# Attention scores as two fp32r matmuls of 128 rows in a hybrid decoder block

## The chip, the cores and the metric

The kernel runs on one core of one Trainium2 chip. The metric is the device time of one execution in microseconds, lower is better. TensorE is PE in the profile (its weight loads are PEld), VectorE is DVE, ScalarE is ACT, GpSimd is POOL, and SyncE, which here only issues transfers, is SP.

## The reference

One decoder block on 512 tokens of width 2048, all in float32: RWKV-7 time mixing and sliding-window attention side by side, merged by gates, then a gated convolutional feed-forward. What the change touches is the attention:

```python
q = rms_norm(q.reshape(B, S, 16, 64), q_gain)
k = rms_norm(k.reshape(B, S, 4, 64), k_gain)
qb = q.reshape(B, nb, 128, 4, 4, 64)          # 4 blocks of 128 tokens, 4 key heads, 4 query heads each
kb, vb = band(k), band(v)                     # each block sees its own 128 keys and the 128 before
scores = jnp.einsum('bnqhgd,bnkhd->bnhgqk', qb, kb) * 64 ** -0.5
scores = jnp.where(valid, scores + alibi, NEG_BIG)
p = jax.nn.softmax(jnp.concatenate([scores, sink], -1), -1)[..., :-1]
o = jnp.einsum('bnhgqk,bnkhd->bnqhgd', p, vb)
```

A score contracts over 64 channels of a head.

## The kernel before

The large matmuls run in fp32r, a form of float32 in which TensorE passes once over the data with a shortened mantissa. Every large operand is therefore split in two: a high part, rounded to fp32r by ACT (`act.activation(hi, src, AF.Copy)`), and a low part, the rest, by DVE (`lo = src - hi`). `load_w` does so for weights (L245 and L246: `whi`, `wlo` from `raw`), `split` for other tiles (L208 and L209 of the kernel before). A projection tile, `ztile`, has 16 chunks of 128 channels with three matmuls each (L262, L263, L264: high times high, high times low, low times high), 128 by 512 elements, into one accumulator `acc`.

The attention stands between 45 and 265 us of the span. It begins with the key and value tiles. `qk_norm` takes a finished accumulator: DVE scales it into `zq` (L410), ACT squares it into `sqq` (L412), four small matmuls sum the squares (`head_stats`, L376), DVE works out the inverse root in a dozen small steps (`rq`), a transpose on PE (L379) and a trip through memory spread it over the rows (`rsb`), and `finish` (L405) multiplies, one tile later, so that the trip is hidden. Its result is `kn` for keys, `qn` for queries: two heads of 64 channels in the two halves of the 128 rows. Each key head is then copied by transfers on ACT's queue (L430) into both halves of its own tile `kd`, so that a query head finds its keys in its own half.

There are four head groups (one key head and four query heads, in two query tiles). `queries(g + 1)` is written ahead of the attention of group g, so that the projections of the next group fill TensorE while the softmax of this one runs; the last group has a gate projection and the following stage's projections instead. For each of the four blocks of a group, L469 makes the scores of its four heads: plain float32, 64 rows (`hs`), in PSUM tiles `scp0` and `scp1`, one for each half of the rows. The program has four such matmuls for a block; a float32 matmul leaves two records in the profile. DVE adds the position bias (L475, `sc`), takes the maximum (L480), ACT exponentiates (L486, `pr`), PE transposes (L495), ACT and DVE copy (L497, L499, `pT`), PE multiplies by the values (L503), DVE scales (L506, `ot`), PE transposes again (L509), ACT copies (L510).

The order on each engine comes from the framework's scheduler, which places instructions by its own estimate of their durations; only what is wrapped in `pin` keeps its written order. POOL's queue carries sums of weights for later stages (L230, `s_o`), each waiting for its first half to land.

Of the kernel before, what the change touches and what calls it, by code (L numbers as in the profile page):

```python
# [8 lines left out]
F32 = mybir.dt.float32  # L9
F32R = mybir.dt.float32r  # L10
F16 = mybir.dt.float16
I32 = mybir.dt.int32
AF = mybir.ActivationFunctionType
ALU = mybir.AluOpType
# [4 lines left out]
P = 128  # L19
S = 512  # L20
NT = S // P
HD = 64
C = 64
NCH = S // C
BLK = 128
# [111 lines left out]
def block_kernel(ctx: ExitStack, tc: tile.TileContext, d: Dims, a: dict, out: bass.AP):  # L137
    nc = tc.nc
    act, dve, pool, pe, sync = nc.scalar, nc.vector, nc.gpsimd, nc.tensor, nc.sync
# [41 lines left out]
    qgs = cstp.tile([P, 1], F32, name="qgs")  # L181
# [25 lines left out]
    def split(hi, lo, src, pin=free):  # L207
        pin(act.activation(hi, src, AF.Copy))  # L208
        pin(dve.tensor_tensor(lo, src, hi.bitcast(F32) if hi.dtype == F32R else hi, op=ALU.subtract))  # L209
# [73 lines left out]
    if True:  # L283
# [107 lines left out]
        with ExitStack() as pt:  # L391
            ap_ = pt.enter_context(tc.tile_pool(name="att", bufs=1, reuse_waits="tile"))
            sps = pt.enter_context(tc.tile_pool(name="sc_ps", bufs=1, space=PSUM, reuse_waits="tile"))
            mps = pt.enter_context(tc.tile_pool(name="mi_ps", bufs=3, space=PSUM, reuse_waits="tile"))

            def small():
                return mps.tile([P, S], F32, name="mi", tag="mi")

            unscaled = []

            def finish():

                if unscaled:
                    dst, z, rb, then = unscaled.pop()
                    pin(dve.tensor_tensor(dst, z, rb, op=ALU.mult))  # L405
                    then()

            def qk_norm(acc, gain, dst, then=lambda: None):
                z = ap_.tile([P, S], F32, name="zq", tag="zq", bufs=3)
                dve.tensor_scalar(z, acc, gain, None, op0=ALU.mult)  # L410
                sq = ap_.tile([P, S], F32, name="sqq", tag="sqq", bufs=2)
                act.activation(sq, acc, AF.Square)  # L412
                ps = small()
                head_stats(ps, sq)
                rs = rsqrt_small(ap_, ps[:, 0 : 2 * NT], 1.0 / HD, RMS_EPS)
                rb = head_rows(ap_, small(), rs, bufs=2)
                finish()
                unscaled.append((dst, z, rb, then))

            NHK = d.KVD // HD  # L420
            kd = [ap_.tile([P, S], F32, name=f"kd{h}") for h in range(NHK)]
            vt = ap_.tile([P, NT, d.KVD], F32, name="vt")
            for t in range(NKV):
                acc = ztile(d.c_ka + t * P)
                kn = ap_.tile([P, S], F32, name="kn", tag="kn", bufs=2)

                def copies(t=t, kn=kn):
                    for h in range(2):
                        for e in range(2):
                            act.dma_start(kd[2 * t + h][e * HD : (e + 1) * HD], kn[h * HD : (h + 1) * HD])  # L430

                qk_norm(acc, col("kg"), kn, copies)
                acc = ztile(d.c_va + t * P)
                vf = ap_.tile([P, S], F32, name="vf", tag="zq", bufs=3)
                act.activation(vf, acc, AF.Copy)
                ps = small().rearrange("p (n c) -> p n c", c=P)
                for b in range(NT):
                    pe.transpose(ps[:, b], vf[:, b * P : (b + 1) * P], ident)
                act.activation(vt[:, :, t * P : (t + 1) * P], ps, AF.Copy)

            GQ = d.HQ // NHK

            def queries(g):
                qn = []
                for j in range(GQ // 2):
                    acc = ztile(d.c_q + (g * GQ // 2 + j) * P)
                    q = ap_.tile([P, S], F32, name=f"qn{j}", tag=f"qn{j}", bufs=2)
                    qk_norm(acc, qgs, q)
                    qn.append(q)
                return qn  # L450

            nxt = queries(0)
            for g in range(NHK):
                qn = nxt
                if g + 1 < NHK:
                    nxt = queries(g + 1)
                else:
                    emit_gate()
                    finish()
                oT = ap_.tile([P, GQ // 2, S], F32, name="oT", tag="oT", bufs=2)  # L460
                for n in range(NT):
                    ts = slice(n * P, (n + 1) * P)
                    k0 = 0 if n else BLK
                    nk = 2 * BLK - k0
                    scp = [sps.tile([P, GQ // 2, 2 * BLK], F32, name=f"scp{e}", tag=f"scp{e}") for e in range(2)]
                    for j in range(GQ // 2):
                        for e in range(2):
                            hs = slice(e * HD, (e + 1) * HD)
                            pe.matmul(scp[e][:, j, k0:], qn[j][hs, ts],  # L469
                                      kd[g][hs, n * P - BLK + k0 : (n + 1) * P], start=True, stop=True)  # L470
                    sc = ap_.tile([P, GQ, 2 * BLK], F32, name="sc", tag="sc", bufs=2)
                    pr_ = ap_.tile([P, GQ, 2 * BLK], F32, name="pr", tag="pr", bufs=2)
                    for h in range(GQ):
                        slope = float(2.0 ** (-8.0 * (g * GQ + h + 1) / d.HQ))
                        dve.scalar_tensor_tensor(sc[:, h, k0:], K["dist"][:, k0:], slope, scp[h % 2][:, h // 2, k0:],  # L475
                                                 op0=ALU.mult, op1=ALU.add)
                    st = ap_.tile([P, 4, GQ], F32, name="st", tag="st", bufs=2)
                    mx, es, den, rc = (st[:, i] for i in range(4))
                    sk = sinkb[:, g * GQ : (g + 1) * GQ]
                    dve.reduce_max(mx, sc[:, :, k0:], axis=AX.X)  # L480
                    dve.tensor_tensor(mx, mx, sk, op=ALU.max)
                    dve.tensor_scalar(mx, mx, -1.0, None, op0=ALU.mult)
                    dve.tensor_tensor(es, sk, mx, op=ALU.add)
                    act.activation(es, es, AF.Exp)
                    for h in range(GQ):
                        act.activation(pr_[:, h, k0:], sc[:, h, k0:], AF.Exp, bias=mx[:, h : h + 1],  # L486
                                       accum_out=den[:, h : h + 1])
                    dve.tensor_tensor(den, den, es, op=ALU.add)
                    dve.reciprocal(rc, den)
                    pT = ap_.tile([P, 2, GQ, BLK], F32, name="pT", tag="pT", bufs=2)  # L490
                    kbs = (0, 1) if n else (1,)
                    for kb in kbs:
                        ps = small().rearrange("p (h c) -> p h c", c=P)
                        for h in range(GQ):
                            pe.transpose(ps[:, h], pr_[:, h, kb * BLK : (kb + 1) * BLK], ident)  # L495
                        if kb:
                            act.activation(pT[:, kb], ps, AF.Copy)  # L497
                        else:
                            dve.tensor_copy(pT[:, kb], ps)  # L499
                    ps = small()[:, : GQ * HD].rearrange("p (h c) -> p h c", c=HD)  # L500
                    for h in range(GQ):
                        for kb in kbs:
                            pe.matmul(ps[:, h], pT[:, kb, h], vt[:, n - 1 + kb, g * HD : (g + 1) * HD],  # L503
                                      start=kb == kbs[0], stop=kb == kbs[-1])
                    ot = ap_.tile([P, GQ, HD], F32, name="ot", tag="ot", bufs=2)
                    dve.tensor_tensor(ot, ps, rc.unsqueeze(2).to_broadcast([P, GQ, HD]), op=ALU.mult)  # L506
                    ps = small()[:, : GQ * HD].rearrange("p (j c) -> p j c", c=P)
                    for j in range(GQ // 2):
                        pe.transpose(ps[:, j], ot[:, 2 * j : 2 * j + 2].rearrange("p h c -> p (h c)"), ident)  # L509
                    act.activation(oT[:, :, ts], ps, AF.Copy)  # L510
                pool.dma_start(
                    o_at_d[g * GQ * HD : (g + 1) * GQ * HD].rearrange("(j p) t -> p j t", p=P), oT)


        with ExitStack() as pr:
# [27 lines left out]
            acc = ztile(d.c_wd)  # L543
# [5 lines left out]
            acc = ztile(d.c_ad)  # L549
# [4 lines left out]
            for i in range(NG):  # L554
                acc = ztile(d.c_gd + i * P)
# [272 lines left out]
            st = early(0)  # L828
# [599 lines left out]
```

## Time and profile before

| | |
|---|---|
| Time, median of 3 runs | 2906.01 us (2901.53 to 2912.75) |
| Profiled execution | 2907.66 us, its span 2905.8 us |
| PE busy | 2850.9 us, 98% of the span |
| DVE, ACT, POOL busy | 1934.3, 1314.6, 228.4 us |
| Granted TensorE clock | 0.996 of full speed |
| Score matmuls (L469) | 128 records, from 127.3 to 251.7 us |

Busy time of PE is a sum over pipelined matmuls whose ends are modelled; how long a matmul holds TensorE is better read from the distance between the starts of neighbours. A row of the timeline gives start, duration, engine, line, operation, output and inputs, tile, shape and how many neighbouring records it joins.

### The profile page before, as it was taken

The numbers are of one execution on the slowest core, as the hardware profiler recorded it, in microseconds if no ns is written. First come the engines' busy times: TensorE is split into PE (matmuls) and PEld (weight loads), VectorE is DVE, ScalarE is ACT, GpSimd is POOL, SyncE is SP. The second block draws the span as 40 slices with busy tenths as digits, with TensorE's granted clock in tenths as the row PEclk, the third lists the DMA queues.
The fourth block names the chain that finished last, engine by engine and source line by source line (L and its number), as shares of the span: only waits on it lengthen the run. The fifth ranks groups of instructions, "written<-read, shape, count | busy, mean of one in ns | idle before, by whom it ended". The sixth has DMA issues, their size and how long they took to land.

```text
span 2905.8 us, 47150 instructions
## 1 busy us (share of the span) xinstructions
PE 2850.9 (98%) x18162; PEld 2491.5 (86%) x18162; DVE 1934.3 (67%) x3314; ACT 1314.6 (45%) x2196; POOL 228.4 (8%) x304
## 2 busy tenths in 40 slices
PE   7999999999999999999999899999999999999999
PEld 6777778878878878788888899999999999888887
DVE  5555676666667665355668778777787777665555
ACT  4344344344334434322356455555555555544444
POOL 0001000000000000111000101110110100000000
PEclk9999999999999999999999999999999999999999
DMA  6855666566665666978787888888888888877775
GB/s 189 213 153 141 171 154 167 147 167 148 160 160 142 161 160 158 282 225 257 270 258 215 224 221 225 241 239 221 235 226 239 241 224 236 308 241 239 259 256 189
DMA packets 223729, 607.38 MB, mean 209 GB/s; under 512 B 24448, under 2 KB 44560, under 8 KB 222480
## 3 DMA queue, kind: packets, MB, share of 16 engines
q1 hardware_dynamic: 156096, 432.92, 45.9%
q0 software_dynamic: 36064, 132.14, 23.9%
q10 hardware_dynamic: 31344, 39.31, 3.9%
q8 instruction: 142, 2.33, 0.3%
q14 instruction: 83, 0.68, 0.1%
HBM read 554.66 MB, written 174.40 MB: 251 GB/s over the span
## 4 chain that ended last, share of the span: by engine, by line
PE 90%; DMA 4%; DVE 4%; issue 1%; ACT 1%; SPq 0%; DVEq 0%; ACTq 0%; POOLq 0%
PE X L1129 17%; PE X L996 10%; PE acc L263 10%; PE acc L262 10%; PE acc L264 10%; PE Y L996 8%; PE Y L1129 8%; PE Z L1129 4%; PE bulk L714 1%; PE bulk L770 1%; PE bulk L740 1%; PE bulk L690 1%; DMA raw<-in_w_up_dram 1%; PE mi L503 1%; PE acc L325 1%
## 5 line engine op out<-in xcount | busy, mean ns | idle before, releaser
L262 PE MATMUL acc<-xhi,whi 128*128 128x512 f32 x1120 | 453.6, 405 | 4.7 <-ACT whi L245 4.7
L264 PE MATMUL acc<-xhi,wlo 128*128 128x512 f32 x1120 | 451.5, 403 | 2.8 <-DVE wlo L246 2.8
L263 PE MATMUL acc<-xlo,whi 128*128 128x512 f32 x1120 | 453.0, 404 | 0.0
L245 ACT ACTIVATE whi<-raw 128x512 fp32r<-128x512 f32 x352 | 220.3, 629 | 499.2 <-PE acc L263 369.0
L246 DVE TENSOR_TENSOR wlo<-raw,whi 128x512 fp32r<-128x512 f32 x352 | 241.4, 689 | 233.5 <-ACT whi L245 227.7
L989 DVE TENSOR_TENSOR wlo<-raw,whi 128x1024 fp32r<-128x1024 f32 x210 | 257.0, 1224 | 205.4 <-ACT whi L988 204.3
L988 ACT ACTIVATE whi<-raw 128x1024 fp32r<-128x1024 f32 x210 | 222.6, 1060 | 291.4 <-PE X L996 152.5
L1129 PE MATMUL X<-b,whi 128*128 128x256 f32 x1472 | 269.1, 283 | 2.2 <-DVE u L1149 0.9
L1129 PE MATMUL X<-t,whi 128*128 128x256 f32 x1408 | 259.9, 285 | 9.9 <-DVE u L1149 9.4
L1112 DVE TENSOR_TENSOR wlo<-raw,whi 128x1024 fp32r<-128x1024 f32 x176 | 215.0, 1222 | 77.3 <-ACT whi L1111 77.0
L1129 PE MATMUL Y<-t,whi 128*128 128x256 f32 x1408 | 257.1, 283 | 0.0
L262 PEld LDWEIGHTS acc<-xhi,whi 128*128 128x128 f32 x1120 | 211.9, 189 | 44.4 <-ACT whi L245 5.5
L264 PEld LDWEIGHTS acc<-xhi,wlo 128*128 128x128 f32 x1120 | 211.9, 189 | 42.0 <-DVE wlo L246 4.0
L263 PEld LDWEIGHTS acc<-xlo,whi 128*128 128x128 f32 x1120 | 211.8, 189 | 37.3 <-issue 1.8
L1111 ACT ACTIVATE whi<-a 128x1024 fp32r<-128x1024 f32 x132 | 139.4, 1056 | 216.5 <-DVE a L1105 214.5
L1129 PEld LDWEIGHTS X<-b,whi 128*128 128x128 f32 x1472 | 229.5, 192 | 3.0 <-issue 2.3
L1129 PEld LDWEIGHTS X<-t,whi 128*128 128x128 f32 x1408 | 221.8, 194 | 10.5 <-DVE u L1149 6.9
L1129 PEld LDWEIGHTS Y<-t,whi 128*128 128x128 f32 x1408 | 219.6, 192 | 0.0
L1129 PE MATMUL X<-b,wlo 128*128 128x256 f32 x736 | 208.5, 283 | 2.1 <-DVE wlo L1112 2.1
L1112 DVE TENSOR_TENSOR wlo<-a,whi 128x1024 fp32r<-128x1024 f32 x132 | 161.7, 1225 | 67.6 <-ACT whi L1111 67.0
L1129 PE MATMUL X<-t,wlo 128*128 128x256 f32 x704 | 200.4, 285 | 0.0
L1129 PE MATMUL Y<-t,wlo 128*128 128x256 f32 x704 | 199.2, 283 | 0.0
(769 smaller groups left out, 6007.1 us busy)
## 6 DMA issues: line engine op xcount, KB each, us to landing
raw<-in_w_up_dram SPq DMA_DIRECT2D x180, 512.0 KB, 4.9
raw<-in_w_z_dram SPq DMA_DIRECT2D x288, 256.0 KB, 4.0
s_dn<-in_w_dn_dram POOLq DMA_DIRECT2D x88, 512.0 KB, 6.5
raw<-in_w_up_dram POOLq DMA_DIRECT2D x88, 512.0 KB, 8.4
raw<-s_dn SPq DMA_DIRECT2D x88, 512.0 KB, 4.1
raw<-in_w_dn_dram SPq DMA_DIRECT2D x66, 512.0 KB, 3.6
a<-in_w_up_dram SPq DMA_DIRECT2D x48, 512.0 KB, 4.4
s_dn<-in_w_dn_dram SPq DMA_DIRECT2D x44, 512.0 KB, 4.7
```

The lines of the kernel that those rows point to most:

```text
L245: pin(act.activation(hi, raw, AF.Copy))
L246: pin(dve.tensor_tensor(lo, raw, hi.bitcast(F32), op=ALU.subtract))
L262: pe.matmul(acc, whi[:, j], xhi[:, k], start=first, stop=False)
L263: pe.matmul(acc, whi[:, j], xlo[:, k], start=False, stop=False)
L264: pe.matmul(acc, wlo[:, j], xhi[:, k], start=False, stop=last)
L325: pin(pe.matmul(heads[i][:, hs], l, r[:, k, hs], start=h == 0 and k + j == 0, stop=k == NK - 1 and j == 2, skip_group_check=True))
L988: act.activation(whi, wr, AF.Copy)
L989: dve.tensor_tensor(wlo, wr, whi.bitcast(F32), op=ALU.subtract)
L996: pe.matmul(dst, l[:, q, ts], r[:, es], start=fst and j == 0, stop=lst and j == 2, skip_group_check=True)
L1111: pin(act.activation(hi, t, AF.Copy))
L1112: pin(dve.tensor_tensor(lo, t, hi.bitcast(F32), op=ALU.subtract))
L1129: pin(pe.matmul(ps, l[:, k], r[:, k], start=start and k + i == 0, stop=last and i == 2, skip_group_check=True))
```

## The change

The scores are computed in fp32r and over all 128 rows. For the queries, each head gets a tile of its own (`q00`, `q10` and so on, shown below as q with a number): the high part in the half of the rows where the head stood, the low part in the other half. For the keys, each head gets two tiles, `khi` and `klo`, with its high part in both halves, and its low part in both halves. One matmul of 128 rows against `khi` then sums (query high + query low) times key high, a second one against `klo` the same times key low, and both accumulate in PSUM. So 64 float32 matmuls of 64 rows become 128 fp32r matmuls of 128 rows with the same 128 and 256 columns. Per query tile there are two copies on ACT and two subtractions on DVE on 64 rows each, and per key tile one split of 128 rows. The copies of the keys go from ACT's queue (8 transfers) to POOL's (16).

```diff
             NHK = d.KVD // HD
-            kd = [ap_.tile([P, S], F32, name=f"kd{h}") for h in range(NHK)]
+            khl = [[ap_.tile([P, S], F32R, name=f"k{e}{h}") for e in ("hi", "lo")] for h in range(NHK)]
...
                 def copies(t=t, kn=kn):
+                    parts = [ap_.tile([P, S], F32R, name=f"kn{e}", tag=f"kn{e}") for e in ("hi", "lo")]
+                    split(*parts, kn)
                     for h in range(2):
-                        for e in range(2):
-                            act.dma_start(kd[2 * t + h][e * HD : (e + 1) * HD], kn[h * HD : (h + 1) * HD])
+                        for i, part in enumerate(parts):
+                            for e in range(2):
+                                pool.dma_start(khl[2 * t + h][i][e * HD : (e + 1) * HD].bitcast(F32),
+                                               part[h * HD : (h + 1) * HD].bitcast(F32))
...
-                    q = ap_.tile([P, S], F32, name=f"qn{j}", tag=f"qn{j}", bufs=2)
-                    qk_norm(acc, qgs, q)
-                    qn.append(q)
+                    q = ap_.tile([P, S], F32, name="qn", tag="qn", bufs=2)
+                    st = [ap_.tile([P, S], F32R, name=f"q{e}{j}", tag=f"q{e}{j}", bufs=2) for e in range(2)]
+
+                    def stacked(q=q, st=st):
+                        for e in range(2):
+                            own, other = (slice(x * HD, (x + 1) * HD) for x in (e, 1 - e))
+                            act.activation(st[e][own], q[own], AF.Copy)
+                            dve.tensor_tensor(st[e][other], q[own], st[e][own].bitcast(F32), op=ALU.subtract)
+
+                    qk_norm(acc, qgs, q, stacked)
+                    qn.append(st)
...
-                            hs = slice(e * HD, (e + 1) * HD)
-                            pe.matmul(scp[e][:, j, k0:], qn[j][hs, ts],
-                                      kd[g][hs, n * P - BLK + k0 : (n + 1) * P], start=True, stop=True)
+                            for i in range(2):
+                                pe.matmul(scp[e][:, j, k0:], qn[j][e][:, ts],
+                                          khl[g][i][:, n * P - BLK + k0 : (n + 1) * P], start=i == 0, stop=i == 1)
```

The scheduler answers with another order. On PE, at the first block of head group 0, before the change (the first L264 is the last matmul of a projection; L262 begins the next one; L376 are the statistics of the projection just finished):

```order
L264 MATMUL acc<-xhi,wlo 128x512
L469 MATMUL scp_1353<-kd_654,qn_977 128x128
L469 MATMUL scp_1354<-kd_654,qn_977 128x128
L469 MATMUL scp_1353<-kd_654,qn_1092 128x128
L469 MATMUL scp_1354<-kd_654,qn_1092 128x128
L262 MATMUL acc<-xhi,whi 128x512
L263 MATMUL acc<-xlo,whi 128x512
L264 MATMUL acc<-xhi,wlo 128x512
L376 MATMUL mi<-cst,sqq 128x2 x4
L262 MATMUL acc<-xhi,whi 128x512
```

and the same place of the changed kernel, where L481 are the scores:

```order
L264 MATMUL acc<-xhi,wlo 128x512
L481 MATMUL scp_1393<-khi_654,q_990 128x128
L481 MATMUL scp_1393<-klo_655,q_990 128x128
L481 MATMUL scp_1394<-khi_654,q_991 128x128
L481 MATMUL scp_1394<-klo_655,q_991 128x128
L481 MATMUL scp_1393<-khi_654,q_1115 128x128
L481 MATMUL scp_1393<-klo_655,q_1115 128x128
L481 MATMUL scp_1394<-khi_654,q_1116 128x128
L376 MATMUL mi<-cst,sqq 128x2 x4
L481 MATMUL scp_1394<-klo_655,q_1116 128x128
L262 MATMUL acc<-xhi,whi 128x512
```

The three projection matmuls that stood ahead of the statistics now come behind them. Groups 1 and 2 have the same pattern.

On ACT, in the softmax of group 2, as the last query tile but one is ready (L457 are the new copies; L498, L509 and L522 of the changed kernel are L486, L497 and L510 of the one before):

```order
L498 ACTIVATE pr,st<-sc,st 128x256
L509 ACTIVATE pT<-mi 128x512
L457 ACTIVATE q_2136<-qn 64x512
L457 ACTIVATE q_2137<-qn 64x512
L498 ACTIVATE pr,st<-sc,st 128x256
L245 ACTIVATE whi<-raw 128x512
L522 ACTIVATE oT<-mi 128x2x128
```

The two copies stand between the exponentials of one block and ahead of a weight chunk's high part; before the change nothing stood there.

On POOL, at the first key tile, as a difference:

```order
 L230 DMA s_o_86<-in_w_o_dram 128x1024
+L433 DMA khi_654<-knhi 64x512 x2
+L433 DMA klo_655<-knlo 64x512 x2
+L433 DMA khi_656<-knhi 64x512 x2
+L433 DMA klo_657<-knlo 64x512 x2
 L230 DMA s_o_94<-in_w_o_dram 128x1024
```

The eight copies of the first key tile come ahead of the fourth weight sum, and those of the second three sums later.

## Prediction

> **What bounds the kernel now.** I read the page first (busy times, the chain that ended last), then the busy time by stretches of 20 us, then TensorE's rows in order of time around the score matmuls.
>
> ```profile
> span 2905.8 us, 47150 instructions
> PE 2850.9 (98%) x18162; PEld 2491.5 (86%) x18162; DVE 1934.3 (67%) x3314; ACT 1314.6 (45%) x2196; POOL 228.4 (8%) x304
> PE 90%; DMA 4%; DVE 4%; issue 1%; ACT 1%; SPq 0%; DVEq 0%; ACTq 0%; POOLq 0%
> ...
> 60.00:80.00 20.00, 19.97 (x94) 15.74 (x92) 9.48 (x32) 6.08 (x10) 1.61 (x2) 1.00 0.67 188
> 120.00:140.00 20.00, 19.96 (x104) 14.38 (x103) 13.60 (x53) 7.41 (x24) 1.62 (x2) 1.00 0.76 204
> 240.00:260.00 20.00, 19.42 (x113) 13.95 (x111) 15.06 (x45) 11.14 (x41) 0.84 (x1) 1.00 0.41 110
> ```
>
> The columns of a stretch are its length, then PE, PEld, DVE, ACT and POOL busy with their counts, the granted clock and the DMA share. The chain runs through TensorE for 90% of the span. The attention stretches (about 127 to 265 us) are no exception: PE is busy 19.96 of 20 us and 19.42 in the worst one, because projection matmuls fill every hole, while DVE has 13.60 and 15.06, ACT 7.41 and 11.14. The clock is 1.00. So a microsecond of TensorE work taken out here is a microsecond of the span, as long as no other engine makes PE wait, and busy time does not tell how much work there is: starts do.
>
> ```profile
> 126.94 0.39 PE L264 MATMUL acc<-xhi,wlo 128*128 128x512 f32 x1
> 127.26 0.71 PE L469 MATMUL scp<-kd,qn 64*128 64x128 f32 x8
> 127.90 0.50 PE L262 MATMUL acc<-xhi,whi 128*128 128x512 f32 x1
> 128.24 0.39 PE L263 MATMUL acc<-xlo,whi 128*128 128x512 f32 x1
> ...
> 128.80 1.05 PE L376 MATMUL mi<-cst,sqq 128*128 128x2 f32 x8
> 129.72 0.48 PE L262 MATMUL acc<-xhi,whi 128*128 128x512 f32 x1
> 130.13 1.13 PE L469 MATMUL scp<-kd,qn 64*128 64x256 f32 x8
> 131.19 0.49 PE L263 MATMUL acc<-xlo,whi 128*128 128x512 f32 x1
> 131.52 0.39 PE L264 MATMUL acc<-xhi,wlo 128*128 128x512 f32 x1
> 131.75 0.40 PE L262 MATMUL acc<-xhi,whi 128*128 128x512 f32 x1
> ...
> 132.68 0.40 PE L263 MATMUL acc<-xlo,whi 128*128 128x512 f32 x1
> 133.00 1.50 PE L469 MATMUL scp<-kd,qn 64*128 64x256 f32 x8
> 134.43 0.50 PE L264 MATMUL acc<-xhi,wlo 128*128 128x512 f32 x1
> 134.77 0.39 PE L262 MATMUL acc<-xhi,whi 128*128 128x512 f32 x1
> ...
> 136.10 0.48 PE L262 MATMUL acc<-xhi,whi 128*128 128x512 f32 x1
> 136.51 1.13 PE L469 MATMUL scp<-kd,qn 64*128 64x256 f32 x4
> 137.57 1.10 PE L503 MATMUL mi<-vt,pT 128*128 128x64 f32 x8
> 138.60 1.13 PE L469 MATMUL scp<-kd,qn 64*128 64x256 f32 x4
> 139.66 0.44 PE L509 MATMUL mi<-ident,ot 128*128 128x128 f32 x2
> ```
>
> This is head group 0, its four query blocks. A block has four score matmuls; each fp32 one leaves two records, hence x8. Three things are to be seen. A projection matmul starts 0.23 us after the one before it (131.52 to 131.75). Around a burst of scores that spacing is 0.32 to 0.41 ahead and 0.33 to 0.34 behind. And the same four matmuls take 1.06 us where the two halves of the rows alternate (130.13), 1.43 where the second half starts late (133.00), and 2 x 1.06 in the last block, where each half has its burst to itself (136.51 and 138.60).
>
> **The change, part by part.**
>
> *Score matmuls removed.* For each burst I take the time from the start of the matmul ahead of it to the start of the second one behind it, less what the matmuls around it take undisturbed (0.23 each; a short record 0.115, from the x8 of 128.80 to 129.72). Block 0: 1.30 - 0.46 = 0.84. Block 1: 1.80 - 0.46 = 1.34. Block 2: 2.09 - 0.46 = 1.63. Block 3, from 136.10 to 139.66: 3.56 - 0.23 - 8 x 0.115 = 2.41. One group 6.2; groups 1 and 2 repeat it, together 18.7. Group 3 is cut into smaller pieces:
>
> ```profile
> 240.59 1.20 PE L469 MATMUL scp<-kd,qn 64*128 64x256 f32 x8
> 242.31 0.33 PE L495 MATMUL mi<-ident,pr 128*128 128x128 f32 x1 [0.52 <-ACT pr L486]
> ...
> 250.12 0.70 PE L469 MATMUL scp<-kd,qn 64*128 64x256 f32 x2
> 250.75 0.66 PE L495 MATMUL mi<-ident,pr 128*128 128x128 f32 x4
> ```
>
> There block 0 is 0.84 again, block 1 takes 1.72 with a wait of 0.52 in it, and blocks 2 and 3 (16 records) stand in pieces of two records at 0.63 each, one pair of them together: about 5.3 with the widened spacings. Group 3 is some 8.0, all scores 26.7 us.
>
> *Score matmuls added.* 128 of 128 rows in fp32r, one record each: 96 with 256 columns, 32 with 128. The trace has the first form:
>
> ```profile
> 50.20 0.28 PE L325 MATMUL acc<-xhi,whi 128*128 128x256 f32 x1
> 50.32 0.28 PE L325 MATMUL acc<-xlo,whi 128*128 128x256 f32 x1
> ```
>
> 0.117 us from start to start over the row of them (0.12 here), so 96 x 0.117 = 11.2. No fp32r matmul of 128 columns is in the trace. From below it is bounded by the short records (0.115), from above by what fp32 would do, two such records, 0.23. I take 0.115, since the 256-column form is already no dearer than a short record: 3.7 us, with 3.7 more at the upper end. Sum 14.9; PE is relieved of 26.7 - 14.9 = 11.8 us. The spacings around the bursts are counted as gone, since the new matmuls have the rows and the kind of the projections.
>
> [...]
>
> *The order around the first block.* In the new order the statistics matmuls of the next query tile (L376) come right behind seven score matmuls; today three projection matmuls stand between. L376 reads a square that ACT makes after DVE has scaled the projection:
>
> ```profile
> 122.20 0.69 DVE L405 TENSOR_TENSOR qn<-zq,rsb 128x512 f32<-128x512 f32 x1 [0.95 <-DMA rsb<-rsd]
> ...
> 127.36 0.75 DVE L410 TENSOR_SCALAR zq<-acc,qgs 128x512 f32<-128x512 f32 x1 [1.59 <-PE acc L264]
> ...
> 128.15 0.60 ACT L412 ACTIVATE sqq<-acc 128x512 f32<-128x512 f32 x1 [0.38 <-DVE zq L410]
> ```
>
> The projection's last matmul starts at 126.94, the square is ready at 128.75. Seven score matmuls end at about 126.94 + 0.23 + 0.8 = 127.98. PE will stand still for about 0.8 us, and everything behind it with it; today about 0.1. That is 0.7 in each of groups 0 to 2, +2.1 us (group 3 has no statistics behind it). Were the 128-column form the dear one, it would fill this hole, so its upper end costs about 1.5 and not 3.7.
>
> *Splits.* For the queries 16 copies on ACT and 16 subtractions on DVE of 64 rows, for the keys 2 and 2 of 128:
>
> ```profile
> L664 DVE TENSOR_TENSOR BKK<-kz,Ei x16: 676/685/691, 336.2 to 1049.6; 64x512 f32<-64x512 f32 x16
> L668 ACT ACTIVATE BV<-vz x16: 620/626/636, 343.8 to 1032.9; 64x512 f32<-64x512 f32 x16
> L245 ACT ACTIVATE whi<-raw x352: 612/632/645, 20.5 to 1395.9; 128x512 fp32r<-128x512 f32 x176
> ```
>
> Half the rows save no time (0.685 and 0.626 for 64 rows, 0.632 for 128), so DVE gets 18 x 0.69 = 12.4 us, ACT 18 x 0.63 = 11.3. DVE's 13.60 of 20 becomes about 15.1: room is left, and PE's projections cover it. Without that cover it would cost up to 12.4. The query is ready at 122.89; two copies and the last subtraction bring that to 124.9, ahead of 127.26. Where the cover is thin is the second tile of a group, in the midst of the softmax: two subtractions stand ahead of the scaling of the output, which a transpose on PE waits for, and two copies ahead of an exponential. I put 1 us in all on that, between 0 and 3.
>
> *Copies of the keys.* Eight transfers of 128 KB go from ACT's queue, sixteen come to POOL's:
>
> ```profile
> 75.54 2.47 ACTq L430 DMA_DIRECT2D kd<-kn  x4
> 78.11 0.63 ACT L245 ACTIVATE whi<-raw 128x512 fp32r<-128x512 f32 x1 [4.04 <-DMA kd<-kn]
> ...
> kd<-kn ACTq DMA_DIRECT2D x8, 128.0 KB, 6.5
> ```
>
> ACT loses 8 x 0.62 = 4.9 us of issuing; its 4.04 us of delay at 78.11 cost PE nothing (19.97 of 20 in that stretch), so I count no gain. POOL takes about 0.81 for an issue (1.62 for two above): keys at 75.5, split 1.3, eight issues 6.5, landing 6.5, that is 90, against 127.26; the second key tile is as early for group 2. POOL's weight sums queue behind for some 6.5 us twice; POOL is 8% busy and nothing near waits on them: nothing.
>
> *Sum.* -11.8 + 2.1 + 1.0 = -8.7 us. The profiled execution took 2907.66 (span 2905.8 and 1.86 around it), so it would be 2899.0; the median shown, 2906.01, is 1.65 below it, so about **2897.5**.
>
> **Rivals.** 0.5% of the time, 14.5 us, is about what a measurement can tell from no change.
>
> [...]
> 2. *Faster by over 0.5%.* No new wait, group 3 loses its own, and the widened spacings at neighbouring matmuls go too: 11.8 + 0.5 + some 2 to 3, 2891. Against: the wait for the square follows from the order.
> 3. *Slower.* ACT works strictly in turn. The new copy waits for the normalised query, that for a broadcast through memory (DVE stood 0.95 us for it at 122.20), and the weights' high parts queue behind the copy. If each of ten tiles held PE up by 3 us, +30 - 8.7: 2927. It decides once a copy is later than at 78.11, where 4.04 us were harmless. Against: the query comes 4.4 us ahead of the scores (122.89 to 127.26).
>
> **How the numbers follow.** Forecast 0.68, the first rival 0.17, the second 0.10, the third 0.05. The scatter of the runs (2901.53 to 2912.75) lets 0.04 of the forecast fall beyond 0.5% and 0.01 of the first rival be slower. So faster 0.14, same 0.80, slower 0.06. The forecast's own ends are -11.8 with no new wait (2894) and -11.8 + 2.1 + 3 + 1.5 = -5.2 (2901). With scatter and the first rival: 2890 to 2907.
>
> **What would show it.** Right: score records of 256 columns 0.12 apart with no widened spacing; a hole of 0.7 to 0.9 us ahead of L376 in three groups; the end of the attention (L509's last) 8 to 9 us earlier and everything behind shifted by that. Wrong: spacings of 0.2 for 128 columns or more; holes ahead of the output's transposes; PE below 19 of 20 in a stretch; or score matmuls waiting for the keys' transfers.

## The result, and the profile after

The changed kernel takes 2897.09 us (median of five runs, 2895.3 to 2899.3) where the kernel before takes 2906.65 (five runs, 2901.53 to 2912.75). The ratio is 0.9971, with a 95% interval from 0.9960 to 0.9982: 9.6 us less; 2897.5 us was forecast. The profiled execution took 2898.65 us.

The page and the stretches of 20 us, to be laid beside those of before (length; PE, PEld, DVE, ACT, POOL busy; granted clock; DMA share and GB/s):

```profile
span 2896.9 us, 47205 instructions
PE 2840.7 (98%) x18162; PEld 2495.9 (86%) x18162; DVE 1945.4 (67%) x3332; ACT 1324.9 (46%) x2214; POOL 236.1 (8%) x320
PE 91%; DVE 4%; DMA 2%; issue 1%; ACT 1%; ACTq 0%; SPq 0%; DVEq 0%; POOLq 0%
```

```profile
120.00:140.00 20.00, 19.23 (x111) 16.36 (x110) 15.37 (x52) 10.44 (x29) 1.61 (x2) 1.00 0.77 211
160.00:180.00 20.00, 18.96 (x98) 15.99 (x98) 14.48 (x53) 9.37 (x26) 1.66 (x2) 0.91 0.63 172
200.00:220.00 20.00, 18.99 (x95) 15.94 (x94) 14.50 (x55) 8.47 (x26) 0.84 (x1) 0.91 0.57 154
240.00:260.00 20.00, 20.00 (x142) 17.77 (x140) 14.53 (x45) 13.24 (x46) 1.11 (x2) 1.00 0.36 98
```

The last group is now full (20.00, before 19.42). The first three groups are emptier than they were, and two stretches show a clock of 0.91. This was not forecast. TensorE's rows in order of time say what lies behind it, first at group 0 (L481 are the scores, L376 the statistics):

```profile
127.50 0.39 PE L264 MATMUL acc<-xhi,wlo 128*128 128x512 f32 x1
127.72 0.22 PE L481 MATMUL scp<-khi,q 128*128 128x128 f32 x1
...
128.23 0.28 PE L481 MATMUL scp<-klo,q 128*128 128x128 f32 x1
128.34 0.27 PE L481 MATMUL scp<-khi,q 128*128 128x128 f32 x1
129.36 1.05 PE L376 MATMUL mi<-cst,sqq 128*128 128x2 f32 x8 [0.74 <-ACT sqq L412]
...
130.94 0.28 PE L481 MATMUL scp<-khi,q 128*128 128x256 f32 x1
131.06 0.28 PE L481 MATMUL scp<-klo,q 128*128 128x256 f32 x1
131.17 0.40 PE L263 MATMUL acc<-xlo,whi 128*128 128x512 f32 x1
131.41 0.28 PE L481 MATMUL scp<-khi,q 128*128 128x256 f32 x1
```

Scores of 128 columns stand 0.11 us apart, those of 256 columns 0.12, and the projection between two bursts takes its plain 0.24 (131.17 to 131.41). The widened spacings of 0.32 to 0.41 are gone. Ahead of L376 PE stands: 0.74 us idle, 1.02 from start to start where 0.11 would do, so a hole of 0.91 (before 0.10). The same hole is at 168.86 and in group 2. What follows it in group 1:

```profile
169.91 0.63 PE L262 MATMUL acc<-xhi,whi 128*128 128x512 f32 x1
170.34 0.42 PE L481 MATMUL scp<-khi,q 128*128 128x256 f32 x1
...
172.48 0.63 PE L264 MATMUL acc<-xhi,wlo 128*128 128x512 f32 x1
172.91 0.63 PE L262 MATMUL acc<-xhi,whi 128*128 128x512 f32 x1
173.33 0.45 PE L263 MATMUL acc<-xlo,whi 128*128 128x512 f32 x1
```

```profile
129.00:133.00 4.00, 3.64 (x24) 3.40 (x25) 3.22 (x18) 0.30 (x2) 0.00 (x0) 1.00 0.91 206
170.00:173.00 3.00, 3.00 (x13) 2.71 (x13) 2.29 (x12) 0.00 (x0) 0.00 (x0) 0.50 0.96 273
211.00:214.00 3.00, 3.00 (x13) 2.72 (x13) 2.29 (x12) 0.00 (x0) 0.00 (x0) 0.50 0.88 182
```

From 170.0 to 173.4 everything is slow: a projection takes 0.43 from start to start and not 0.23, a score 0.21 and not 0.12. The granted clock (third column from the right) is 0.50 there and again behind the hole of group 2, but 1.00 behind that of group 0. Each of the two (from 170.01 and from 210.97 us) is 3.41 us long in the records of the clock and costs half of that, 1.7 us. Below, a slow stretch is one at half clock.

I call the time from the start of the first score matmul to the start of the output's last transpose the attention. It took 138.1 us before (127.3 to 265.4) and 133.6 after (127.7 to 261.3). The stage behind it begins at 309.8 instead of 315.0, 5.2 us earlier. The span is 8.9 shorter.

### The profile page after: what moved, and what is told of

It is laid out like the page before. It is cut to its first block, busy times and chain, and to the rows that moved or that the text cites. A ratio compares the mean times of both kernels' runs of the same rounds, so it can differ in the third digit from the quotient of the medians.

```text
span 2896.9 us, 47205 instructions
## 1 busy us (share of the span) xinstructions
PE 2840.7 (98%) x18162; PEld 2495.9 (86%) x18162; DVE 1945.4 (67%) x3332; ACT 1324.9 (46%) x2214; POOL 236.1 (8%) x320
## 4 chain that ended last, share of the span: by engine, by line
PE 91%; DVE 4%; DMA 2%; issue 1%; ACT 1%; ACTq 0%; SPq 0%; DVEq 0%; POOLq 0%
PE X L1141 17%; PE X L1008 11%; PE acc L262 10%; PE acc L263 10%; PE acc L264 10%; PE Y L1008 9%; PE Y L1141 8%; PE Z L1141 4%; PE bulk L726 1%; PE bulk L782 1%; PE bulk L752 1%; PE bulk L702 1%; PE mi L515 1%; DMA raw<-in_w_z_dram 1%; PE acc L325 1%
## 5 line engine op out<-in xcount | busy, mean ns | idle before, releaser
L262 PE MATMUL acc<-xhi,whi 128*128 128x512 f32 x1120 | 453.3, 405 | 3.6 <-ACT whi L245 3.6
L263 PE MATMUL acc<-xlo,whi 128*128 128x512 f32 x1120 | 452.8, 404 | 0.0
L264 PE MATMUL acc<-xhi,wlo 128*128 128x512 f32 x1120 | 451.2, 403 | 1.5 <-DVE wlo L246 1.5
L262 PEld LDWEIGHTS acc<-xhi,whi 128*128 128x128 f32 x1120 | 211.9, 189 | 42.7 <-ACT whi L245 4.4
L264 PEld LDWEIGHTS acc<-xhi,wlo 128*128 128x128 f32 x1120 | 211.9, 189 | 39.7 <-DVE wlo L246 2.8
L263 PEld LDWEIGHTS acc<-xlo,whi 128*128 128x128 f32 x1120 | 212.0, 189 | 36.0 <-issue 0.5
```

Of the source, the lines that this page charges most:

```text
L262: pe.matmul(acc, whi[:, j], xhi[:, k], start=first, stop=False)
L263: pe.matmul(acc, whi[:, j], xlo[:, k], start=False, stop=False)
L264: pe.matmul(acc, wlo[:, j], xhi[:, k], start=False, stop=last)
```

## The experiments

The theory at this point (theory A): TensorE bounds the attention, the hole stands because block 0's scores are now shorter than the way to the square, and the half-clock windows come from the hole. The rival: VectorE or ScalarE sets the pace of the softmax, and the hole is only where that shows. The kernel before stood at a median of 2907.26 us beside e1 to e4 and of 2906.25 beside e5 to e7.

| kernel | us | ratio, 95% | attention, us | next stage begins | half clock behind groups |
|---|---|---|---|---|---|
| before | 2906.65 | | 138.1 | 315.0 | none |
| changed | 2897.09 | 0.9971 (0.9960 to 0.9982) | 133.6 | 309.8 | 1, 2 |
| e1_wide0 | 2895.54 | 0.9959 (0.9947 to 0.9971) | 127.7 | 304.3 | none |
| e2_again | 2899.26 | 0.9974 (0.9964 to 0.9984) | 133.5 | 309.5 | 1, 2 |
| e3_hionly | 2890.49 | 0.9943 (0.9931 to 0.9955) | 125.5 | 297.6 | none |
| e4_pairs | 2953.71 | 1.0158 (1.0145 to 1.0172) | 199.7 | 362.8 | 75 us from 265 on |
| e5_onetile | 2905.56 | 0.9997 (0.9986 to 1.0007) | 139.1 | 315.4 | none |
| e6_splits | 2905.68 | 1.0002 (0.9994 to 1.0011) | 138.9 | 315.6 | none |
| e7_actq | 2909.60 | 1.0013 (1.0004 to 1.0023) | 133.6 | 316.3 | 1, 2; 6.8 us at 109 |

**Taking the hole away (e1_wide0), and the changed kernel again (e2_again).** Block 0 of each group is computed over 256 key columns, of which the second 128 are not used; this makes its eight score matmuls hardly dearer, and the scheduler puts projections ahead of L376 again.

```
-  pe.matmul(scp[e][:, j, k0:], qn[j][e][:, ts],
-            khl[g][i][:, n * P - BLK + k0 : (n + 1) * P], ...)
+  c0 = max(n * P - BLK, 0)
+  pe.matmul(scp[e][:, j], qn[j][e][:, ts], khl[g][i][:, c0 : c0 + 2 * BLK], ...)
```

> The changed kernel, but the first block of each group makes its scores over 256 key columns instead of 128 (the second half is not read), so that the scheduler again puts three projection matmuls ahead of the statistics (L376). Theory A: the hole of 0.9 us ahead of L376 in groups 0 to 2 costs the changed kernel 2.5 us, and it is also what brings the half-clock windows at 169.7 and 210.7 us (1.7 us each); without it no hole, no window in the attention, score time about 15.5 us, and 2891.5 us, ratio 0.995. Theory B: the windows at half clock come by their own timing and have nothing to do with the hole: the holes go (-2.5), the windows stay: 2894.5, ratio 0.996. Theory C: the hole is filled elsewhere and costs nothing: 2897, as the changed kernel.

> The changed kernel once more, unchanged. Ratio 0.9970 again. Theory A: the holes of about 0.9 us ahead of L376 return in all three groups, since the order makes them; the half-clock windows depend on where a window of 3.41 us begins, so they may fall on groups 1 and 2 together (their distance, 40.96 us, is twelve windows), on group 0, or on none. Theory B: they stand where they stood, at 169.7 and 210.7.

Group 1 of e1_wide0 (scores L482), and its stretch:

```profile
166.25 0.28 PE L482 MATMUL scp<-khi,q 128*128 128x256 f32 x1
...
167.08 0.28 PE L482 MATMUL scp<-klo,q 128*128 128x256 f32 x1
167.19 0.40 PE L262 MATMUL acc<-xhi,whi 128*128 128x512 f32 x1
167.43 0.40 PE L263 MATMUL acc<-xlo,whi 128*128 128x512 f32 x1
167.66 0.40 PE L264 MATMUL acc<-xhi,wlo 128*128 128x512 f32 x1
167.90 1.05 PE L376 MATMUL mi<-cst,sqq 128*128 128x2 f32 x8
```

```profile
160.00:180.00 20.00, 19.74 (x118) 17.05 (x118) 15.82 (x53) 11.19 (x31) 1.66 (x2) 1.00 0.68 168
```

Eight wider matmuls take 0.94 us, the statistics wait for nothing, the clock is 1.00, and the attention is 5.9 us shorter than in the changed kernel. The three holes (3 x 0.81 more than before, 2.4) and the two slow stretches (3.4) make 5.8. More work of TensorE gave a shorter time. The unchanged repeat has the hole and the slow stretches at the same places. The totals alone would not decide: e1_wide0's 2895.54 us lies nearer to theory B's 2894.5 than to theory A's 2891.5, and 3.7 below e2_again's 2899.26. The trace decides: no hole, no slow stretch in the attention, and the next stage begins 5.2 us earlier than in e2_again. This is also the fastest version that computes all: 11.7 us below before.

**Half of the new matmuls (e3_hionly).** The keys' low part is left out of the scores (`for i in range(1)`).

> The changed kernel without the matmul against the low part of the keys: scores leave that part out, 64 score matmuls instead of 128. It prices score work on TensorE. Theory A (TensorE bounds the attention): 48 x 0.118 + 16 x 0.112 = 7.5 us less work, and the statistics again have three projection matmuls ahead, so the holes (2.5) and their clock windows (3.4) go as well: 2897 - 7.5 - 2.5 = 2887 with the windows, 2883.5 without. Theory D (the softmax on DVE and ACT bounds the attention, so that less TensorE work is given back): no more than 3 us less, 2894.

The total, 2890.49 us, lies between theory A's 2883.5 without slow stretches and theory D's 2894, so again the trace has to tell. The next stage begins 6.7 us earlier than in e1_wide0, for 64 matmuls less (64 x 0.117 = 7.5) and three remaining holes of 0.4 to 0.5. Work taken from TensorE comes out nearly whole: theory A. That the holes would go as well was a miss. (The attention itself ends only 2.6 us earlier; 4.1 us of projections that stood behind it, 49.2 us and now 45.1, went in.) ACT's square is waited for, but less (0.34 idle at 166.14), and no slow stretch follows in the attention.

**What pairing the two halves is worth (e4_pairs, e5_onetile).** In e4_pairs the score matmuls of before are held in program order, so that the halves alternate (`pin(pe.matmul(scp[e]...))`).

> The kernel before with its float32 score matmuls kept in written order, so that the two halves of the rows alternate in every block. [...] Theory A: each block then costs what the paired ones cost, 0.85 + 3 x 1.35 a group = 19.6 in all against 27.3, so about 7 us less than before if nothing else waits: 2899; the pinned order also holds a block's scores behind the end of the block before, which may cost waits of some us: 2899 to 2904. Theory E (alternation does not overlap, the spread of 1.06 to 2.12 has another cause): bursts of 2.1 us in all blocks, 2915.

That was a miss by 50 us, and not for the price of the pairs. Rows of blocks 1 and 2 in group 0, two stretches, and what PE waited for between 260 and 340 us:

```profile
141.04 1.13 PE L469 MATMUL scp<-kd,qn 64*128 64x256 f32 x8
...
153.16 1.13 PE L469 MATMUL scp<-kd,qn 64*128 64x256 f32 x8
```

```profile
200.00:220.00 20.00, 20.00 (x118) 15.69 (x117) 9.30 (x23) 8.61 (x27) 1.61 (x2) 1.00 0.62 165
280.00:300.00 20.00, 13.87 (x56) 9.91 (x54) 6.17 (x22) 6.87 (x28) 0.77 (x1) 0.50 0.07 26
```

```profile
PE mi L495 <- ACT pr L486: 15.0, 5, 3.8
```

Every block of the first three groups is one burst, at 0.85 + 3 x 1.27 us by the accounting of the prediction, 4.66 a group. So full pairing would make all scores 18.6 us. But the held order spread the blocks over the projections. At 265 us the third group's last block and the whole fourth group still stood ahead, with no projection left beside them: PE waited for the exponentials, and its clock was halved for 75 us. Where the halves alternate, four score matmuls take 1.06 us (141.04 to 142.10 here, 130.13 to 131.19 in the kernel before), against 2 x 1.06 where each half has its own burst (136.51 and 138.60 in the kernel before).

In e5_onetile both halves lie in one scores tile and nothing is held.

```
-  scp = [sps.tile([P, GQ // 2, 2 * BLK], F32, name=f"scp{e}", ...) for e in range(2)]
+  scp = sps.tile([P, 2, GQ // 2, 2 * BLK], F32, name="scp", tag="scp")
```

> The kernel before with one scores tile for both halves instead of two, so that the four score matmuls of a block come free together and the two halves alternate without any instruction being pinned; fp32, 64 rows, no splits. Theory A (TensorE bounds the attention; pairing is worth only what the alternating bursts show): blocks 0 to 3 cost 0.84, 1.3, 1.5, 1.6 us, about 5.2 a group instead of 6.2, and group 3 loses about 2 of its 8.0, so -4 to -5 us, 2902.5. [...] Rival (the holes between projections hide it): no change, 2907. It tells how much of the change's gain was to be had without fp32r: the changed kernel gained 9.6.

```profile
140.76 0.38 PE L495 MATMUL mi<-ident,pr 128*128 128x128 f32 x2
141.08 0.70 PE L469 MATMUL scp<-kd,qn 64*128 64x256 f32 x2
141.70 0.66 PE L495 MATMUL mi<-ident,pr 128*128 128x128 f32 x4
142.29 0.70 PE L469 MATMUL scp<-kd,qn 64*128 64x256 f32 x4
```

No gain, a miss. Block 1 is paired at 1.27, but the last block came out in pieces (the rows above), and block 2 as three matmuls and a single one, 2.1 us together (before 1.63). A single matmul of two records costs 0.62 alone and 0.76 to 0.83 with the spacings at its ends, hardly less than the pair at 142.29 (0.89). All scores take 26.4 us (before 27.3). With 64 rows the order decided; with 128 rows it mattered less: in the last group of the changed kernel a score of 256 columns takes 0.12 us in a burst (240.01 to 240.13) and 0.12 to 0.20 between transposes (241.51 to 241.63, 241.66 to 241.86).

**The splits alone (e6_splits).** The kernel before, with the 16 copies and 16 subtractions of the queries added and not used.

> The kernel before plus the queries' splits alone (16 copies on ScalarE and 16 subtractions on VectorE of 64 rows); scores go on as before and do not use them. Theory A (the splits lie beside projections): within 1 us of 2907, at most +3. Rival (VectorE or ScalarE sets the attention): +5 to +12, 2912 to 2919, with holes in TensorE's rows ahead of the output's transposes.

No change: the attention is 0.8 us longer, the next stage begins 0.6 later. What PE waited for from 120 to 270 us is one entry:

```profile
PE mi L379 <- DVE rq L199: 0.4, 1, 0.4
```

**The keys' copies on the other queue (e7_actq).** The changed kernel with `act.dma_start` for the sixteen transfers.

> The changed kernel with the sixteen transfers of the keys' parts issued on ScalarE's queue instead of GpSimd's; TensorE's order is the same. Theory A (the keys are 30 us early, so the queue does not matter): 2897, within 1 us. Rival (ScalarE strictly in turn: the weights' high parts queue behind sixteen issues of 0.6 us): +2 to +5, 2899 to 2902, with spacings of projections over 0.23 around 80 us. The hole of 0.9 us ahead of the statistics stays; whether half-clock windows follow it in groups 1 and 2 depends on where the windows of 3.41 us fall in this execution.

ACT in order of time, and the PE row that waited:

```profile
99.70 1.40 ACTq L433 DMA_DIRECT2D khi<-knhi  x2
101.20 1.36 ACTq L433 DMA_DIRECT2D klo<-knlo  x2
105.93 1.61 ACTq L433 DMA_DIRECT2D khi<-knhi  x2
107.58 1.25 ACTq L433 DMA_DIRECT2D klo<-knlo  x2
108.88 0.60 ACT L412 ACTIVATE sqq<-acc 128x512 f32<-128x512 f32 x1 [9.21 <-DMA khi<-knhi]
```

```profile
109.53 1.65 PE L376 MATMUL mi<-cst,sqq 128*128 128x2 f32 x7 [2.72 <-ACT sqq L412]
```

The eight issues of the second key tile hold ACT from 99.7 to 108.9 (3.4 us of it between the fourth issue and the fifth), the square behind them comes late, PE stands 2.7 us, and 6.8 us at half clock follow. Ratio to before 1.0013, some 12 us above the changed kernel, of which 6.5 stand ahead of the next stage's beginning: theory A was wrong here, and the rival right in kind, and too low. On ScalarE's queue the change would have gained nothing. The same hole of 0.91 stays in the three groups.

**The place of the slow stretches (e8_phase_a, e8_phase_b, e9_shift8, e10_shift15).** Open was why the same hole is followed by half clock in groups 1 and 2 and not in group 0. The first two runs are the changed kernel, the others add projection matmuls, eight and fifteen (`for _ in range(extra * first): pe.matmul(acc, whi[:, j], xhi[:, k], start=True, stop=True)`). In the traces they stand at 65 to 70 us, so some 60 us ahead of the first scores and not 25.

> The changed kernel once more, for the place of the half-clock windows. They are 3.41 us long and stand on a fixed grid whose place against the kernel differs from execution to execution. Theory: TensorE's clock is halved for one window after a window that holds both the 0.9 us hole and the 0.9 us of two-column matmuls behind it (1.8 us together); if a window's edge cuts these 1.8 us near their middle, no halving follows. Group 1 and group 2 stand 41.0 us apart, 12 windows, so both fall alike; group 0 stands 11.5 windows ahead and falls the other way. So an execution has half clock behind groups 1 and 2 (as both profiles so far), or behind group 0 alone, or nowhere, and its attention (first score matmul to the output's last transpose) takes 133.5, some 131.8 or 130.1 us. Rival (halving follows the hole itself, wherever the grid stands): the same two places every time.

> As the run ahead of it: another execution, another place of the grid. At a random place about half of the executions should have half clock behind groups 1 and 2.

> The changed kernel with eight projection matmuls issued once more than needed (into a tile that is then overwritten) some 25 us ahead of the first scores: everything behind them shifts by 8 x 0.227 = 1.8 us. In the four profiles so far the hole and the two-column matmuls behind it stood at 0.8 to 3.2 us of a window of 3.41 us in groups 1 and 2 (whole, halved next) and at 2.2 to 4.9 in group 0 (cut by the window's end, not halved). Theory (the halving needs the 1.8 us whole inside one window, and the grid of windows stands about where it stood): groups 1 and 2 are now cut and show no half clock, group 0 is whole and shows it; attention 131.8 us instead of 133.5, so that the total is about what it was in spite of 1.8 us more work. Rivals: halving follows groups 1 and 2 wherever the grid is, 133.5; or the grid moves along with the work, 133.5.

> As the run ahead, with fifteen extra matmuls, 15 x 0.227 = 3.4 us, one whole window. Theory: the pattern of the changed kernel comes back, half clock behind groups 1 and 2 and none behind group 0, attention 133.5 us. Rival (any shift takes the halving away): 130.1 or 131.8.

Their single times (2901.22, 2900.44, 2903.74 and 2901.75 us) are too few to compare; the traces tell the places. e8_phase_a, e8_phase_b and e10_shift15 have half clock behind groups 1 and 2 again (attention 133.6 in each). The first two do not part the theory from its rival, since the grid fell alike in all four profiles of the changed kernel: group 1's hole began 0.8 to 1.6 us behind a window's start. e10_shift15 rules out that any shift takes the halving away, but is no test of a whole window: its attention begins only 1.7 us later than the changed kernel's, because its start lacks the slow stretch that the changed kernel has at 23 us. e9_shift8 has half clock behind all three groups (135.4). Group 0 of e9_shift8 (L378 are the statistics there, L264 and L265 the projections that are L262 and L263 elsewhere), and its stretch:

```profile
131.79 1.05 PE L378 MATMUL mi<-cst,sqq 128*128 128x2 f32 x8 [0.74 <-ACT sqq L414]
...
132.85 0.45 PE L264 MATMUL acc<-xhi,whi 128*128 128x512 f32 x1
...
133.79 0.63 PE L265 MATMUL acc<-xlo,whi 128*128 128x512 f32 x1
```

```profile
133.40:136.80 3.40, 3.40 (x14) 2.92 (x13) 3.00 (x18) 0.88 (x5) 0.00 (x0) 0.50 1.02 243
```

All slow stretches of one execution start at whole multiples of 3.413 us from each other, which gives the grid of windows. In the changed kernel's profile they start at 23.24, 170.01, 210.97, 1190.60, 1589.96 and 1637.74 us, which are 43, 12, 287, 117 and 14 times 3.413 apart; in the profile of before at 23.96, 334.57, 1198.15 and 1645.29, which are 91, 253 and 131 times. Counted from the start of the span, the grid's first window begins at 2.76 us in the one and at 0.07 in the other. Against it I placed the 1.8 us of hole and two-column matmuls, 21 times in seven profiles with the hole. In 15 they lie whole inside a window (from 0.48 to 1.59 us behind its start): a slow stretch follows in all 15. In 6 they run over a window's end (from 1.95 to 3.04): in none. In three of these 6 (from 1.95 to 2.27) the 0.9 us of standing still lie whole inside the window, and yet nothing follows. e9_shift8 moved group 0 from the one kind to the other, as expected. That groups 1 and 2 would then be cut was a miss: group 0's own slow stretch added 1.7 us to the 1.8 of the shift, which is one whole window, and they stood where they had stood. So in these 21 places half clock went with the whole 1.8 us in one window, and not with the hole alone or the group. e3_hionly, with holes of 0.5, has none, but there all three also run over a window's end, so it does not tell what a smaller hole does. At most 1.5 of the 1.8 us lay inside one window where nothing followed.

The plain waits behind the attention show the same. At the weights' low part (L264) and in the next stage's `bulk` matmuls, twelve profiles (all but e4_pairs) have 23 waits of over 1 us between 300 and 350 us. A slow stretch follows three of them, which had 1.88, 1.89 and 2.76 us inside one window. It follows none of the other 20, which had at most 1.79 us inside one window. The longest wait of all is among these 20, since a window's end cut it into 1.1 and 1.8 (e8_phase_a):

```profile
329.95 0.50 PE L264 MATMUL acc<-xhi,wlo 128*128 128x512 f32 x1 [2.89 <-DVE wlo L246]
```

So by the idle times of the profile, the longest plain wait inside one window without half clock behind it was 1.79 us, and the shortest with it 1.88.

## Why the prediction was right, and where it was not

The total is right, in part by luck: the attention gave half of what was forecast, and the rest came from behind it. By the attention's length:

| term | forecast | shown |
|---|---|---|
| scores | -11.8 | -11.1 (27.3 to 16.2, e1_wide0, where no hole disturbs them) |
| hole ahead of L376 | +2.1 | +2.4 (3 x 0.81) |
| DVE's waits in the softmax, splits | +1.0 | +0.8 (e6_splits) |
| keys' copies on POOL | 0 | 0 (no score waits for them; first of them issued at 76.9) |
| half clock behind the hole | not in the sum | +3.4 (2 x 1.7) |
| sum | -8.7 | -4.5; measured 133.6 - 138.1 = -4.5 (by the next stage's beginning -5.2) |

- *Scores.* Right: 128 columns at 0.11 us, the lower of the two bounds, 256 at 0.12, no widened spacing left. The scores of before were rightly priced burst by burst (26.7): they cost 27.3, and 18.6 only where every block is paired (e4_pairs). e4_pairs shows that the row of block 1 told the price of pairing truly (1.34, there 1.27), and that the kernel before could not have it for nothing.
- *The hole.* Right in place, in cause and in size (0.7 to 0.9 forecast, 0.81 more than before).
- *The step that failed* is "PE will stand still for about 0.8 us, and everything behind it with it". It counted the hole at its own length. Two of the three holes also cost a window at half clock, 1.7 us each, more than the hole. Neither the sum nor a rival had it, and "PE below 19 of 20", named as a sign of a wrong forecast, came true at 160 and 200 us.
- *The attention's end* came 4.1 us earlier, where 8 to 9 were forecast. So "everything behind shifted by that" was wrong too: the span shrank by 8.9, and some 3.7 of it stand behind the next stage's beginning. Part of that is at the weights' low part, first the row of before, then of after:

```profile
334.47 0.73 PE L264 MATMUL acc<-xhi,wlo 128*128 128x512 f32 x1 [2.76 <-DVE wlo L246]
```

```profile
327.98 0.50 PE L264 MATMUL acc<-xhi,wlo 128*128 128x512 f32 x1 [1.51 <-DVE wlo L246]
```

  Before, the wait lies whole in one window and half clock followed it (0.73 and not 0.50); after, a window's end at 327.03 cuts it. But e6_splits, whose attention is that of before, waits 1.80 there with no half clock behind it, and e8_phase_a, the changed kernel, waits 2.89 there, so this differs from execution to execution and is not the change's. The changed kernel's `bulk` matmuls then wait 1.89 at 338.21, where before has 0.28, so that only some 1.3 of the 3.7 have come about by there. The four profiles of the changed kernel (the changed one, e2_again, e8_phase_a, e8_phase_b) have spans of 2896.9 to 2899.4, with the attention alike to 0.1 us. The medians say 8.0 to 9.6 us of gain for an attention that gave 4.5 to 5.2. What makes the other 3 to 4 us is not settled: e1_wide0's 11.7 against its 10.4 to 10.7 leaves only 1. Scatter can make much of it, since the intervals of the two ratios reach down to gains of 5.2 and 4.7 us. The number was hit partly because this offset the unforeseen 3.4, and that was luck.
- *Rivals.* The upper end of the range, 2907, and 0.17 of the chances count on a first rival of 2904 to 2906, the gain given back. No run shows the gain given back: the changed kernel's medians are 2897.09 and 2899.26. What PE waited for from 120 to 270 us after the change, in all, times, longest:

```profile
PE mi L376 <- ACT sqq L412: 2.2, 3, 0.7
PE mi L379 <- DVE rq L199: 0.6, 2, 0.3
PE mi L515 <- DVE pT L511: 0.3, 1, 0.3
PE mi L521 <- DVE ot L518: 0.2, 1, 0.2
```

  The softmax (the last two) makes 0.5 us, where the sum has 1. The second (2891) asked for no new wait. e1_wide0, which has none, gained 11.7 us and not the 15 of that rival. Of the third, that ACT's work stood in line behind what was issued ahead of it is true of the keys' copies, which the change had put on POOL: with them on its queue ACT computed nothing for 9.21 us ahead of the square at 108.88 (e7_actq), and before the change for 4.04 ahead of a weight's high part at 78.11. The queries' copies, which the third rival meant, held nothing up (e6_splits).

## What to carry to other kernels

Count a hole on the busiest engine together with the small work around it, and against the clock: 0.9 us of waiting and 0.9 us of two-column matmuls cost 2.5 us and not 0.8 where they fell into one window of the clock, and cheap extra columns that fill the hole beat both. When matmuls get shorter, look for the wait that they used to cover. Price a small matmul by starts between its neighbours and not alone, since with half the rows 0.2 us of a piece of 0.83 were its ends (e5_onetile).

## What the hardware showed

- Half clock came in stretches of 3.41 us or a multiple (6.83 at 1637.74 in the changed kernel, 10.24 at 1645.29 before), on a grid of 3.413 us that is fixed within an execution: 15 of 15 after 1.8 us of hole and two-column matmuls in one window, 0 of 6 when a window's end cut them. Plain waits had it behind 1.88 us or more in one window (3 of 3) and not behind 1.79 or less (0 of 20). Where PE waited at every step it held for 75 us (e4_pairs).
- In e9_shift8 the eight extra matmuls (1.8 us) moved the later groups by about twice that, since the first group's slow stretch added another 1.7.
- An fp32r matmul of 128 rows took 0.11 us for 128 columns and 0.12 for 256 (128.23 to 128.34 and 130.94 to 131.06 in the changed kernel), so the second 128 columns cost 0.01. It leaves one record (L481: 128 for 128 matmuls), a float32 one two (L469: 128 for 64).
